# Weights that wait in the caches' buffers, squares added pair by pair, and a new order of streams in a one-core decoder layer

## The chip, the core and the metric

The kernel runs on one core of a Trainium2 chip. The metric is the time of one execution on the device, in microseconds. The kernel before takes 557.04 us (median of three runs, 556.88 to 557.81).

## The reference

One layer of a decoder with two token mixers on 256 new prompt tokens and 64 sampled tokens (8 requests of 8 tokens, each with 1024 cached tokens in pages of 128), 1024 channels wide, everything in fp32. Cut to what matters:

```python
h = rms_norm(x, g_mix)
qa, ka, va, qs, ks, vs, ga, gs = split(h @ w_in)          # 512 x6, 1024 x2
qa, ka = rope(qa), rope(ka)
o_a = moba(qa, past_a + ka, past_a + va)     # softmax over the own block and the best 3 blocks of 256
o_s = stick_breaking(qs, past_s + ks, past_s + vs)
merged = sigmoid(ga) * (o_a @ w_branch_moba) + sigmoid(gs) * (o_s @ w_branch_sb)
x = x + merged @ w_out
h2 = rms_norm(x, g_ffn)
x = x + (silu(h2 @ w_gate) * (h2 @ w_up)) @ w_down        # 2816 wide
y = rms_norm(x, g_final)
return y, ka, va, ks, vs
```

## The kernel before

Channels lie on the 128 partitions, the 320 tokens along the free dimension, so the input x is a tile of 128 x 8 x 320 and a weight for 128 output channels is 128 x 1024, 0.5 MB. Every dense product is made three times in a reduced form of fp32: x and each weight are split into a high part (ACT, a cast, L152, tile wh) and a low part (DVE, a subtraction, L153, tile wl), and TensorE adds up high x high, low x high and high x low (`acc`, L185, and `products`, L344), 24 matmuls of 320 columns for one tile of 128 output channels (named dps). A raw weight comes by DMA from the SP queue into one of three buffers (wr, L157), and its parts lie in three buffers each.

The first norm is not applied to x but to the products. `load_x` loads x in four pieces of two k-tiles and the first two weights in halves, splits them as they land, squares x (ACT, L316), adds the squares (DVE, L319, L321) and `rsqrt` sums them over the channels with TensorE (cs, L261), takes the root (ACT, L262) and a Newton step (DVE, L263 to L267). `first_norm` spreads the result over the partitions with TensorE (rb, L275). The first two dense tiles are computed side by side, in four steps of two k-tiles, and wait with the third (`NORM`) until the norm is there; their rotation (ACT, L363) and the next tiles follow.

Until some 265 us the kernel mixes six streams of work: d (dense tiles of q, k and v and the first branch product), g (gates), s (scores against the cached keys, S, L571, then the own scores, own, L620, zo, L622, and the softmax, pown, L645), a (values, po, L696), e (ends) and p (attention of the prompt). The string `ORDER` says which stream takes the next step; TensorE, POOL and SP run in the order in which the program is written, while a scheduler orders ACT and DVE. After every step `Loads.feed` issues what has become possible: it splits waiting weights as long as fewer than three split ones are unused, and starts the loads that stand next in the order of need, weights on SP and keys on SP (kr, L533, four DMAs of 0.25 MB), values on POOL (vr, L541, an indirect DMA of 1 MB). Keys and values share a ring of eight buffers (tag cr) of 1 MB. Before it issues a page of values, POOL reads an element of the key tile that was loaded second to last (seen, L540), so that pages do not overtake keys.

Behind that come the gated branches, the output projection with the second norm, the feed-forward part and `last_norm`: for each half of the tokens it sums the squares with TensorE (rb, L861), makes r on ACT (L870, L871) and DVE (L875, L876), copies r to PSUM (rstd, L877), multiplies the x that was scaled by g_final (xg, L873 for the last tile) by r in three products (L865), on DVE or POOL, and stores each (L866).

Of the kernel before, what the change touches and what calls it, by code (L numbers as in the profile page):

```python
# [10 lines left out]
ALU = mybir.AluOpType  # L11
# [27 lines left out]
FIRST = "wwwwc"  # L39
# [13 lines left out]
    "dddddddsdddsdddsdaspaddsadasegaddaapedsapdpsggdaapepaaddgpds"  # L53
    "spepdgddpsagasapggegapaapgpsseggpggpdsagdasaaedgaaded"
# [7 lines left out]
class Loads:  # L62
# [4 lines left out]
    def __init__(self, needs, parts, split):  # L67
# [4 lines left out]
        self.ready = 0  # L72
# [8 lines left out]

    def split_one(self):

        self.got["w"].append(self.parts())
        self.split(*self.got["w"][-1], self.raw.pop(0))
        self.ready += 1

# [7 lines left out]
    def feed(self):  # L95

        while self.raw and self.ready - self.used["w"] < WB:
            self.split_one()
        left, held, begun = [], set(), 0
        for kind, load in self.todo:  # L100
            if kind == "c":
                free = self.begun["c"] - self.used["c"] < RB and begun < PACE
            else:
                free = self.begun["w"] - self.ready < WR
# [35 lines left out]
class Net:  # L140
# [14 lines left out]
    def load_weights(self, src, n):  # L155
        raw = self.wpool.tile([P, 1024], F32, name=self.uid("wr"), tag="wr", bufs=WR)
# [121 lines left out]
    def load_x(self):  # L278
# [10 lines left out]
        w = [self.wpool.tile([P, 1024], F32, name=self.uid("wr"), tag="wr", bufs=WR) for i in range(2)]  # L289
        parts = [self.weight_parts() for i in range(2)]  # L290
        load_w = lambda i, h: nc.sync.dma_start(w[i][:, half[h]], self.I["w_in"][i][:, 4 * h:4 * h + 4])
        load_x = lambda g: nc.sync.dma_start(x[:, 2 * g:2 * g + 2], self.I["x"][:, 2 * g:2 * g + 2])
        nc.scalar.dma_start(self.small, self.I["c_small"])
        for h in range(2):
            load_x(2 * h)
            load_w(0, h)
            load_w(1, h)
# [3 lines left out]
        self.loads.begin(FIRST[:2])  # L301

        nc.scalar.activation(self.warm, self.ones[:, 0:1], AF.Sqrt)
        for k in range(KD):
# [3 lines left out]
            if k % 4 < 2:  # L308
                nc.scalar.activation(parts[k % 4][0][:, half[h]], w[k % 4][:, half[h]], AF.Copy)
# [25 lines left out]
    def products(self, tiles, n):  # L335
# [3 lines left out]
        for k in range(0, KD, n):  # L339
            for low in range(2):  # L340
                for w, ps in zip(ws, pss):
# [727 lines left out]
```

## Time and profile before

| what | value |
|---|---|
| median of the runs | 557.04 us (556.88 to 557.81) |
| profiled execution | 557.35 us, of which its span 555.6 us |
| granted clock of TensorE, mean | 0.996 |
| TensorE busy | 540.8 us (97%) |
| DVE, ACT, POOL busy | 328.7, 270.4, 50.4 us |
| DMA | 138.86 MB, mean 250 GB/s |
| chain that ended last | TensorE 88%, DMA 5%, DVE 3%, ACT 3% |

TensorE is busy nearly all the time, and what is not its work lies in a few waits and at the two ends. Busy time counts a matmul up to its modelled end, so that a share of 97% does not say that matmuls follow each other as closely as they can: from 265 to 545 us they start 0.146 us apart (1913 in 280.00 us). A line number in a row is that of the kernel before.

### The profile page before, as it was taken

What the parts mean: (1) busy time and instruction counts of PE and PEld (TensorE: products, weight loads), DVE (VectorE), ACT (ScalarE), POOL (GpSimd) and SP (SyncE); (2) the same over time, 40 slices, a digit from 0 to 9 for tenths busy, and PEclk for the clock granted to TensorE, in tenths of its full rate; (3) what the DMA queues carried; (4) which work ended last, traced back from release to release, by engine and by line L of the source; (5) the groups of instructions that cost most, each with busy time, mean ns of one, the idle gap of its engine ahead of it and who ended that gap; (6) DMA issues with size and microseconds to landing.
All of it is one profiled execution on the core that took longest, in us unless ns stands there. A gap on an engine that the chain in (4) does not pass through costs nothing.

```text
span 555.6 us, 10933 instructions
## 1 busy us (share of the span) xinstructions
PE 540.8 (97%) x4254; PEld 492.1 (89%) x4254; DVE 328.7 (59%) x599; ACT 270.4 (49%) x488; POOL 50.4 (9%) x74
## 2 busy tenths in 40 slices
PE   8899999999999999999999999999999999999993
PEld 6788677878878778878999999999999999999993
DVE  5786655464468537663877666555555565443432
ACT  6894555526675346532545464444443333353421
POOL 0001211150034202320000000000000000000001
PEclk9999999999999999999999999999999999999998
DMA  6999999999799999995585444445544444545512
GB/s 229 380 390 368 352 384 416 399 415 403 251 354 360 422 392 339 403 377 189 171 323 172 144 140 152 152 152 152 150 145 149 148 146 137 154 145 142 169 36 94
DMA packets 45427, 138.86 MB, mean 250 GB/s; under 512 B 5184, under 2 KB 7488, under 8 KB 41152
## 3 DMA queue, kind: packets, MB, share of 16 engines
q1 hardware_dynamic: 40336, 104.06, 54.5%
q0 software_dynamic: 4608, 33.56, 14.9%
q8 instruction: 33, 0.54, 0.4%
q10 hardware_dynamic: 432, 0.56, 0.3%
q14 instruction: 18, 0.15, 0.1%
HBM read 134.22 MB, written 3.93 MB: 249 GB/s over the span
## 4 chain that ended last, share of the span: by engine, by line
PE 88%; DMA 5%; DVE 3%; ACT 3%; issue 1%; POOL 0%; DVEq 0%; SPq 0%; ACTq 0%; POOLq 0%
PE dps L185 56%; PE dps L344 16%; PE po L696 5%; PE S L571 4%; DMA wr<-in_w_in 2%; DMA vr<-in_cv,small 2%; PE dps L388 1%; PE dps L518 1%; PE dps L463 1%; PE tp L504 1%; DVE wl L153 1%; PE tp L672 1%; ACT wh L152 1%; DMA small<-in_c_small 1%; ACT sq L316 0%
## 5 line engine op out<-in xcount | busy, mean ns | idle before, releaser
L152 ACT ACTIVATE wh<-wr 128x1024 fp32r<-128x1024 f32 (+1 forms) x122 | 127.1, 1045 | 180.1 <-issue 105.3
L153 DVE TENSOR_TENSOR wl<-wr,wh 128x1024 fp32r<-128x1024 f32 (+1 forms) x122 | 146.9, 1205 | 67.7 <-ACT wh L152 67.1
L185 PE MATMUL dps<-x1h,wh 128*128 128x320 f32 x352 | 109.0, 310 | 0.0
L185 PE MATMUL dps<-x1l,wh 128*128 128x320 f32 x352 | 108.8, 309 | 0.0
L185 PE MATMUL dps<-x1h,wl 128*128 128x320 f32 x352 | 108.8, 309 | 0.0
L344 PE MATMUL dps<-xs,wh 128*128 128x320 f32 x256 | 78.0, 318 | 0.3 <-ACT xs L306 0.3
L344 PE MATMUL dps<-xl,wh 128*128 128x320 f32 x256 | 76.1, 310 | 0.2 <-DVE xl L307 0.2
L185 PEld LDWEIGHTS dps<-x1h,wh 128*128 128x128 f32 x352 | 66.1, 188 | 0.1
L185 PEld LDWEIGHTS dps<-x1l,wh 128*128 128x128 f32 x352 | 66.1, 188 | 0.0
L185 PEld LDWEIGHTS dps<-x1h,wl 128*128 128x128 f32 x352 | 66.1, 188 | 0.0
L185 PE MATMUL dps<-fl,wh 128*128 128x320 f32 x176 | 54.4, 309 | 0.0
L185 PE MATMUL dps<-fh,wl 128*128 128x320 f32 x176 | 54.4, 309 | 0.0
L185 PE MATMUL dps<-fh,wh 128*128 128x320 f32 x176 | 54.4, 309 | 0.0
L344 PEld LDWEIGHTS dps<-xs,wh 128*128 128x128 f32 x256 | 48.1, 188 | 3.9 <-issue 2.4
L344 PEld LDWEIGHTS dps<-xl,wh 128*128 128x128 f32 x256 | 48.1, 188 | 1.0 <-DVE xl L307 0.6
L344 PE MATMUL dps<-xs,wl 128*128 128x320 f32 x256 | 43.1, 309 | 0.0
L344 PEld LDWEIGHTS dps<-xs,wl 128*128 128x128 f32 x256 | 39.0, 188 | 0.0
L541 POOL DMA_INDIRECT vr<-in_cv,small x32 | 36.0, 1124 | 19.1 <-PE po L696 8.6
L696 PE MATMUL po<-vr,pt 128*32 128x256 f32 x512 | 32.0, 381 | 1.1 <-DMA vr<-in_cv,small 1.1
L185 PEld LDWEIGHTS dps<-fh,wh 128*128 128x128 f32 x176 | 33.0, 188 | 0.0
L185 PEld LDWEIGHTS dps<-fl,wh 128*128 128x128 f32 x176 | 33.0, 188 | 0.0
L185 PEld LDWEIGHTS dps<-fh,wl 128*128 128x128 f32 x176 | 33.0, 188 | 0.0
(202 smaller groups left out, 845.8 us busy)
## 6 DMA issues: line engine op xcount, KB each, us to landing
kr<-in_ck SPq DMA_DIRECT2D x128, 256.0 KB
wr<-in_w_ff SPq DMA_DIRECT2D x44, 512.0 KB
wr<-in_w_in SPq DMA_DIRECT2D x30, 512.0 KB
wr<-in_w_down SPq DMA_DIRECT2D x16, 448.0 KB
wr<-in_w_v SPq DMA_DIRECT2D x8, 512.0 KB
wr<-in_w_b SPq DMA_DIRECT2D x8, 512.0 KB
wr<-in_w_out SPq DMA_DIRECT2D x8, 512.0 KB
wr<-in_w_down SPq DMA_DIRECT2D x8, 512.0 KB
```

Source lines behind the costliest of these rows:

```text
L152: self.nc.scalar.activation(hi, raw, AF.Copy)
L153: self.nc.vector.tensor_tensor(lo, raw, r32(hi), ALU.subtract)
L185: nc.tensor.matmul(ps, w, x, start=first and i == 0, stop=last and i == len(todo) - 1)
L344: self.nc.tensor.matmul(ps, a, x, start=k + low + i == 0, stop=low == 1 and k + n == KD and i == n - 1)
L388: nc.tensor.matmul(ps, self.xs[:, k], w[k][j], start=k + j == 0, stop=k + j == KD)
L463: nc.tensor.matmul(S[e][:, i], q[r, 2 * u + i, half * P:half * P + P], k[r, 2 * u + i, half * P:NP_], start=True, stop=True)
L504: nc.tensor.transpose(tp[:, i * P:(i + 1) * P], src, self.ident)
L518: nc.tensor.matmul(po[r, i, :NP_ if kt else P], t["v"][:, kt, c0:c0 + HD], mv, start=kt == 1, stop=kt == 0)
L541: self.nc.gpsimd.indirect_dma_start(out=raw.rearrange("p a b -> p (a b)"), out_offset=None, in_=self.I[f"cv{br}"], in_offset=bass.Indirect ...
L571: nc.tensor.matmul(S[r], self.block(QS, x, hp), raw[x][:, :, hp * P:(hp + 1) * P], start=i == 0, stop=i == 1)
L672: nc.tensor.transpose(tp[:, i * P:(i + 1) * P], pf[:, 4 * g + i], self.ident)
L696: nc.tensor.matmul(po[r], PT[j][:, r], v[:, c:c + 256], start=j == 0, stop=j == 8)
```

## The change

It has five parts. First, `FIRST` and `begin_two`: two pairs of early weights (the third and fourth of w_in, and the sixth and seventh) are loaded into buffers of the caches' ring, two weights in one buffer (wc), beside the three of their own; a buffer goes back to the ring when both weights in it are split. The constants (cosine, sine, identity, diagonal) are issued between them. Second, the squares: two of the four are made among the first casts, and they are added pair by pair, in three additions of 128 x 640. Third, x lies in DRAM as four contiguous pieces, and is read so again later. Fourth, a new `ORDER`, and queries of the second branch are made when that is possible at another tile. Fifth, the end: DVE scales the last tile, the products are in another order, and all stores but the last go over the SP queue.

```diff
-FIRST = "wwwwc"
+FIRST = "WwkccWw"
+SIDE = 2
+SQUARES = (), (), (), (0,), (), (), (), (2,), (), (4, 6)
...
-    "dddddddsdddsdddsdaspaddsadasegaddaapedsapdpsggdaapepaaddgpds"
-    "spepdgddpsagasapggegapaapgpsseggpggpdsagdasaaedgaaded"
+    "ddddddddsdsdddsdadspdddasapeddasdgpdspaasegaggaaapdepaddpdsa"
+    "spepdgdpsagpdapaseggapgpaagsseggpggpdsagddasaaegaaded"
...
+    def begin_two(self, tile):
+        self.begun["c"] += 1
+        for raw in [tile[:, 2 * i:2 * i + 2].rearrange("p a b -> p (a b)") for i in range(2)]:
+            i = [kind for kind, _ in self.todo].index("w")
+            self.todo.pop(i)[1](raw)
+            self.raw.append(raw)
+            self.guests.append(raw)
...
     def split_one(self):
...
+        if any(raw is g for g in self.guests):
+            self.away += 1
+            self.used["c"] += self.away % 2 == 0
...
-        load_x = lambda g: nc.sync.dma_start(x[:, 2 * g:2 * g + 2], self.I["x"][:, 2 * g:2 * g + 2])
+        load_x = lambda g: nc.sync.dma_start(x[:, 2 * g:2 * g + 2], self.I["x"][g])
...
-        self.loads.begin(FIRST[:2])
+        for c in FIRST:
+            if c == "k":
+                self.constants3()
+            elif c == "W":
+                self.loads.begin_two(self.craw.tile([P, 4, 512], F32, name=self.uid("wc"), tag="cr", bufs=RB))
+            else:
+                self.loads.begin(c)
...
+        def square(k):
+            nc.scalar.activation(sq[:, k:k + 2], x[:, k:k + 2], AF.Square)
+            if k:
+                nc.vector.tensor_add(sq[:, :2], sq[:, :2], sq[:, k:k + 2])
         for k in range(KD):
...
+            for j in SQUARES[k]:
+                square(j)
         self.loads.are_split(parts)
-        self.loads.split_one()
-        for k in range(0, KD, 2):
-            nc.scalar.activation(sq[:, k:k + 2], x[:, k:k + 2], AF.Square)
+        if SIDE < WB:
+            self.loads.split_one()
+        for j in SQUARES[9]:
+            square(j)
...
-        for n in (4, 2):
-            nc.vector.tensor_add(sq[:, :n], sq[:, :n], sq[:, n:2 * n])
...
+            e = KD - 1
+            nc.vector.tensor_scalar(xg[:, e], self.x1[:, e], self.g_fin[:, e:e + 1], None, op0=ALU.mult)
             for h in range(2):
                 nc.scalar.activation(r[h], ps[h], AF.Abs_reciprocal_sqrt, scale=1.0 / D)
                 nc.scalar.activation(w[h][0], r[h], AF.Square)
-            e = KD - 1
-            nc.scalar.activation(xg[:, e], self.x1[:, e], AF.Copy, scale=self.g_fin[:, e:e + 1])
             for h in range(2):
...
-                product(nc.gpsimd, nc.scalar, h, 5, 8, r[h])
+                product(nc.vector, nc.sync, h, 0, 2, rb[h] if h else r[h])
                 if h == 0:
-                    product(nc.vector, nc.sync, 0, 0, 2, r[0])
-            for h, e0, e1 in (0, 2, 5), (1, 0, 2), (1, 2, 5):
-                product(nc.vector, nc.sync, h, e0, e1, rb[h])
+                    product(nc.vector, nc.sync, h, 2, 5, rb[h])
+                product(nc.gpsimd, nc.sync, h, 5, 8, r[h])
+            product(nc.vector, nc.scalar, 1, 2, 5, rb[1])
```

How the instructions stand is seen best from the rows of an engine. ACT at the start, before (xs is the cast of x, sq a square, wh a weight's high part, rot a rotation, rtok the root of the norm):

```order
L306 ACTIVATE xs<-x_105,small 128x320 x2
L152 ACTIVATE wh_151<-wr_122 128x1024
L316 ACTIVATE sq_106<-x_105 128x640 x4
L317 ACTIVATE xs<-xl 128x8x64
L152 ACTIVATE wh_258<-wr_124 128x1024
L363 ACTIVATE rot_388<-dps_208 32x320 x4
L363 ACTIVATE rot_396<-dps_209 32x320 x4
L152 ACTIVATE wh_262<-wr_174 128x1024
L152 ACTIVATE wh_335<-wr_176 128x1024
L262 ACTIVATE rtok<-cs_323,small 128x3
L152 ACTIVATE wh_424<-wr_266 128x1024
```

And after:

```order
L342 ACTIVATE wh_111<-wr_108 128x512
L338 ACTIVATE xs<-x_105,small 128x320 x2
L333 ACTIVATE sq_106<-x_105 128x640
L173 ACTIVATE wh_192<-wc_122 128x1024
L333 ACTIVATE sq_106<-x_105 128x640 x2
L355 ACTIVATE xs<-xl 128x8x64
L173 ACTIVATE wh_275<-wc_122 128x1024
L401 ACTIVATE rot_403<-dps_225 32x320 x4
L401 ACTIVATE rot_411<-dps_226 32x320 x4
L173 ACTIVATE wh_279<-wr_125 128x1024
L284 ACTIVATE rtok<-cs_340,small 128x3
```

One square has moved between the casts of x (above these rows) and one behind the last of them, the other two stand behind the first whole weight (wh_192), and one whole weight (wh_279) instead of two stands between the rotations and the root.

TensorE, before, where the second half of the first value product begins (S are the scores of the next pair, po the value product):

```order
L344 MATMUL dps_1092<-xs,wl_843 128x320 x8
L571 MATMUL S_1126<-kr_768,QS_195 32x512 x2
L571 MATMUL S_1126<-kr_802,QS_195 32x512 x2
...
L696 MATMUL po_1031<-vr_893,pt_935 32x256 x2
L696 MATMUL po_1031<-vr_916,pt_935 32x256 x2
```

After, where the same value product begins, with its first half:

```order
L382 MATMUL dps_1100<-xs,wl_846 128x320 x8
L735 MATMUL po_1132<-vr_654,pt_907 32x256 x2
L735 MATMUL po_1132<-vr_693,pt_907 32x256 x2
...
L610 MATMUL S_1165<-kr_741,QS_212 32x512 x2
L610 MATMUL S_1165<-kr_781,QS_212 32x512 x2
...
L735 MATMUL po_1132<-vr_866,pt_914 32x256 x2
L735 MATMUL po_1132<-vr_895,pt_914 32x256 x2
```

Before, the first half came two dense tiles earlier; after, the first half stands behind these tiles, and only the scores stand between the halves.

ACT, before, at the second v weights (v and vt are the copies of v, QS that of the queries, pown the exponential of the own scores, p that of the others):

```order
L383 ACTIVATE v_204<-dps_699,rtok 128x256
L602 ACTIVATE QS_195<-qT_202 64x4x2x8
L152 ACTIVATE wh_687<-wr_534 128x1024
L390 ACTIVATE vt_799<-dps_782,rtok 64x256
L152 ACTIVATE wh_691<-wr_601 128x1024
L645 ACTIVATE pown_749,st_604<-zo_745,st_604 64x8 x2
L647 ACTIVATE p_603,st_604<-S_605,st_604 128x2x8x16 x2
```

And after:

```order
L421 ACTIVATE v_221<-dps_657,rtok 128x256
L173 ACTIVATE wh_635<-wr_494 128x1024
L641 ACTIVATE QS_212<-qT_219 64x4x2x8
L421 ACTIVATE v_221<-dps_755,rtok 128x256
L684 ACTIVATE pown_722,st_642<-zo_718,st_642 64x8
L173 ACTIVATE wh_683<-wr_547 128x1024
L684 ACTIVATE pown_722,st_642<-zo_718,st_642 64x8
L686 ACTIVATE p_641,st_642<-S_643,st_642 128x2x8x16 x2
```

The high part of the fourth v weight, wh_687 before and wh_683 after, stood two rows and another weight in front of pown and now stands behind its first instruction.

## Rows read from the trace of the kernel before

**Rows 1.** Two stretches: busy time of each engine, granted clock, DMA share, rate.

```profile
core 0: us, PE busy (x) PEld busy (x) DVE busy (x) ACT busy (x) POOL busy (x), PEclk, DMA share, GB/s
95.00:140.00 45.00, 45.00 (x438) 36.38 (x440) 22.90 (x56) 21.46 (x48) 9.96 (x16) 1.00 1.02 405
265.00:545.00 280.00, 280.00 (x1913) 279.80 (x1912) 163.69 (x242) 120.29 (x173) 0.00 (x0) 1.00 0.48 151
```

**Rows 2.** TensorE's waits: line, for whom, us in total, times, longest.

```profile
PE cs L261 <- DVE sq L321: 1.4, 1, 1.4
PE po L696 <- DMA vr<-in_cv,small: 1.1, 2, 0.8
...
PE rb L275 <- PE dps L344: 0.8, 1, 0.8
```

**Rows 3.** ACT at the start, in order of time: start, us, operation, [idle before].

```profile
7.83 1.47 ACT L306 ACTIVATE xs<-x,small 128x320 fp32r<-128x320 f32 x3 [1.17 <-DMA x<-in_x]
...
12.93 2.60 ACT L316 ACTIVATE sq<-x 128x640 f32<-128x640 f32 x4
...
20.56 2.01 ACT L152 ACTIVATE wh<-wr 128x1024 fp32r<-128x1024 f32 x2
...
26.39 1.28 ACT L327 ACT_TABLE_LOAD   x1
```

**Rows 4.** DVE in order of time at the start.

```profile
15.57 1.49 DVE L319 TENSOR_TENSOR sq<-sq 128x1280 f32<-128x1280 f32 x1 [1.28 <-ACT sq L316]
...
18.18 0.82 DVE L319 TENSOR_TENSOR sq<-sq 128x640 f32<-128x640 f32 x1
19.03 0.49 DVE L321 TENSOR_TENSOR sq<-sq 128x320 f32<-128x320 f32 x1
...
21.66 2.36 DVE L153 TENSOR_TENSOR wl<-wr,wh 128x1024 fp32r<-128x1024 f32 x2 [1.03 <-ACT wh L152]
```

**Rows 5.** TensorE in order of time, value products and the tiles behind them.

```profile
77.48 0.60 PE L696 MATMUL po<-vr,pt 128*32 128x256 f32 x4
...
80.70 0.41 PE L344 MATMUL dps<-xs,wh 128*128 128x320 f32 x1
...
91.37 0.63 PE L696 MATMUL po<-vr,pt 128*32 128x256 f32 x4
...
94.63 0.41 PE L344 MATMUL dps<-xs,wh 128*128 128x320 f32 x1
...
101.86 1.93 PE L696 MATMUL po<-vr,pt 128*32 128x256 f32 x32
...
104.16 0.33 PE L664 MATMUL tp<-ident,pown 128*128 128x128 f32 x1
```

**Rows 6.** POOL in order of time, before the late value pages.

```profile
65.06 1.40 POOL L540 COPY seen<-kr 1x1 f32<-1x1 f32 x1 [13.69 <-DMA kr<-in_ck]
```

**Rows 7.** The chain of waits from 60 to 95 us: start us, us, what.

```profile
82.06 10.68 DMA vr<-in_cv,small
```

**Rows 8.** The tail in order of time.

```profile
547.61 0.33 DVE L875 SCALAR_TENSOR_TENSOR v<-w,rb 128x160 f32<-128x160 f32 x1 [1.47 <-ACT w L871]
...
548.05 0.55 ACT L873 ACTIVATE xg<-x,small 128x320 f32<-128x320 f32 x1
548.34 0.49 DVE L865 TENSOR_TENSOR out<-xg,r 128x320 f32<-128x320 f32 x1
...
548.73 2.35 POOL L865 TENSOR_TENSOR out<-xg,r 128x480 f32<-128x480 f32 x2 [301.33 <-ACT xg L873]
```

**Rows 9.** Two stretches of the tail.

```profile
550.50:551.00 0.50, 0.00 (x0) 0.00 (x0) 0.29 (x1) 0.18 (x1) 0.50 (x1) 1.00 0.30 115
551.00:554.00 3.00, 0.00 (x0) 0.00 (x0) 0.76 (x2) 0.00 (x0) 0.08 (x1) 0.60 0.97 363
```

**Rows 10.** DVE and ACT around the own scores of the first pair.

```profile
51.72 0.17 DVE L622 TENSOR_TENSOR zo<-own,small 128x8 f32<-128x8 f32 x1 [0.57 <-PE dps L388]
...
55.13 0.30 ACT L645 ACTIVATE pown<-zo,st 64x8 f32<-64x8 f32 x1 [0.51 <-DVE st L643]
```

More of the change, by code (lines that the diff above doesn't have):

```diff
@@ L95, in feed @@
     def feed(self):
+        ready = self.ready - self.away
         while self.raw and self.ready - self.used["w"] < WB:
             self.split_one()
+        if not WLAG:
+            ready = self.ready - self.away
         left, held, begun = [], set(), 0
@@ L103, in feed @@
             else:
-                free = self.begun["w"] - self.ready < WR
+                free = self.begun["w"] - ready < WR
             if free and kind not in held:
@@ L153, in split, with load_weights @@
         self.nc.vector.tensor_tensor(lo, raw, r32(hi), ALU.subtract)
-    def load_weights(self, src, n):
-        raw = self.wpool.tile([P, 1024], F32, name=self.uid("wr"), tag="wr", bufs=WR)
+    def load_weights(self, src, n, raw=None):
+        if raw is None:
+            raw = self.wpool.tile([P, 1024], F32, name=self.uid("wr"), tag="wr", bufs=WR)
         self.nc.sync.dma_start(raw[:, :n], src)
@@ L288, in load_x @@
         half = slice(0, 512), slice(512, 1024)
-        w = [self.wpool.tile([P, 1024], F32, name=self.uid("wr"), tag="wr", bufs=WR) for i in range(2)]
-        parts = [self.weight_parts() for i in range(2)]
+        w = [self.wpool.tile([P, 1024], F32, name=self.uid("wr"), tag="wr", bufs=WR) for i in range(SIDE)]
+        parts = [self.weight_parts() for i in range(SIDE)]
         load_w = lambda i, h: nc.sync.dma_start(w[i][:, half[h]], self.I["w_in"][i][:, 4 * h:4 * h + 4])
-        load_x = lambda g: nc.sync.dma_start(x[:, 2 * g:2 * g + 2], self.I["x"][:, 2 * g:2 * g + 2])
+        load_x = lambda g: nc.sync.dma_start(x[:, 2 * g:2 * g + 2], self.I["x"][g])
         nc.scalar.dma_start(self.small, self.I["c_small"])
@@ L295, in load_x @@
             load_x(2 * h)
-            load_w(0, h)
-            load_w(1, h)
+            for i in range(SIDE):
+                load_w(i, h)
             load_x(2 * h + 1)
@@ L308, in load_x @@
             if k % 4 < 2:
-                nc.scalar.activation(parts[k % 4][0][:, half[h]], w[k % 4][:, half[h]], AF.Copy)
+                for i in range(1, SIDE) if k % 4 else [0]:
+                    nc.scalar.activation(parts[i][0][:, half[h]], w[i][:, half[h]], AF.Copy)
             if k % 4 == 1:
@@ L339, in products @@
         for k in range(0, KD, n):
-            for low in range(2):
-                for w, ps in zip(ws, pss):
-                    pairs = [(w[low][:, j], x[:, j]) for j in range(k, k + n) for x in (self.xh, self.xl)[:2 - low]]
-                    for i, (a, x) in enumerate(pairs):
-                        self.nc.tensor.matmul(ps, a, x, start=k + low + i == 0, stop=low == 1 and k + n == KD and i == n - 1)
+            steps = [(low, i) for low in range(2) for i in range(len(tiles))]
+            for low, i in steps if k + n < KD else sorted(steps, key=lambda v: v[1]):
+                w, ps = ws[i], pss[i]
+                pairs = [(w[low][:, j], x[:, j]) for j in range(k, k + n) for x in (self.xh, self.xl)[:2 - low]]
+                for j, (a, x) in enumerate(pairs):
+                    self.nc.tensor.matmul(ps, a, x, start=k + low + j == 0, stop=low == 1 and k + n == KD and j == n - 1)
         return pss
@@ L409, in gen_qk @@
             if f == 0:
-                side_by_side = self.products([0, 1], 2)
-            todo.append((which, hp, side_by_side.pop(0) if f < 2 else self.project(f)))
+                side_by_side = self.products(range(SIDE), 2)
+            todo.append((which, hp, side_by_side.pop(0) if f < SIDE else self.project(f)))
             if f < NORM:
@@ L767, in out_proj @@
         self.rstd2 = rstd = q.tile([P, T], F32, name="rstd2")
-        nc.sync.dma_start(x1, I["x"])
+        for g in range(4):
+            nc.sync.dma_start(x1[:, 2 * g:2 * g + 2], I["x"][g])
         acc = self.acc1 = q.tile([P, 1, T], F32, name="acc1")
@@ L962, in build @@
                 self.page_rows()
-                self.constants3()
-                self.loads.begin(FIRST[2:])
                 self.work = mid.enter_context(pool("work"))
```

17 lines of the change are left out of this document (11 added, 6 removed).

## The prediction

> **What bounds the kernel now.** I read the stretches first, then TensorE's waits, then the order in time at the places that the waits name. From 265 to 545 us TensorE has no gap at all, 280.00 us for 1913 matmuls, 0.146 each; from 95 to 140 us it has none either, while the DMA engines are full at 405 GB/s [rows 1]. So the time is TensorE's work plus its few waits plus the tail behind 545 us, and a change that keeps the matmuls can only win or lose waits. The list of waits has, of those that the change touches, the column sums behind the squares (1.4 us), the value pages (1.1 us on TensorE's own list) and the broadcast of the norm (0.8 us, put down to TensorE, in truth behind a chain on ACT and DVE) [rows 2]. I price these places and the tail, and then look for what the new order could hold up.
>
> **The start: squares and norm.** Before, ACT makes all four squares only from 12.93 us on, in 2.60 us, 0.65 each [rows 3]. DVE then adds 128x1280 (15.57, 1.49 us), a weight's low part comes between, then 128x640 (18.18, 0.82) and 128x320 (19.03, 0.49) [rows 4]. The sum is there at 19.52; the third tile was through at 17.9. After, the first square stands behind the cast of k=3 and the second behind that of k=7. ACT has work without a gap from 7.83 us to the squares, so its casts of the second half come a square later, 0.65: the two tiles side by side end some 0.6 later, the third begins near 15.0 instead of 14.4 and ends near 18.5 (24 matmuls are 3.5). The adds become three of 128x640 (0.82 each) instead of 1.49 + 0.82, 0.15 more, but the first lies beside ACT's next weight. On DVE I get: first add 13.05 to 13.87, low part 14.1 to 15.3 (1.2 each, 2.36 for two [rows 4]), two adds to 16.95, low part 17.05 to 18.25, last sum 18.75. The column sums start 0.8 earlier and wait 0.2 instead of 1.4.
>
> What decides is the next link, the norm. Before, ACT casts two weights (20.56, 2.01 us) between the rotations and the root [rows 3], and DVE makes two low parts (21.66, 2.36 us) before the Newton step [rows 4]. After, one cast and one low part stand there. Up to the rotations' end ACT has the same work as before. One cast and one low part less bring the end of the low parts from 24.0 to about 22.7, and the broadcast 1.3 us earlier than 24.9. The fourth tile ends near 22.9, so a wait of 0.7 stays. **Term 1: -1.3 us**, bounds -0.9 (the square in front of the casts costs more than its row) and -2.2 (with rival a).
>
> Two pairs of weights go into cache buffers. They lend two of the eight until about 18 and 30 us; the first product with keys comes behind the eighth tile, past 36, so I cost the loan at nothing. Uncovered it would be a tile of keys, 1.05 MB at 405 GB/s, 2.6 us.
>
> **The value pages.** The page's 1.1 us understates them. An undisturbed second half of a value product (40 matmuls) takes 2.30 us to the next tile, 101.86 to 104.16, so a first half (32) takes 1.84. The second half at 77.48 took until 80.70, 3.22, and the first half at 91.37 until 94.63, 3.26 [rows 5]: 0.92 + 1.42 = 2.3 us lost. The pages were late because POOL, which issues them, stood 13.69 us until 65.06 for a tile of keys [rows 6], and because a page then needs up to 10.68 us from issue to landing [rows 7]. In the new order the first value products stand behind three more dense tiles, near 75 instead of 66.6 us; the second half follows at 78.7, and the next come as a double at 108. I counted the megabytes that must have landed before each tile (0.52 a weight, 2.1 a pair of tiles of keys or values) against 390 GB/s: the two tiles that waited had 24.1 and 29.4 MB ahead of them and some 11 us of slack in that count; after, the second half has 24.7 MB at a time 3.5 us later, and the double 35.7 MB with 14 us. The buffers of its four tiles come free by 81, 27 us ahead. I take both waits as gone: **term 2: -2.3 us**, bounds 0 and -2.3.
>
> **The tail.** Before, ACT scales the last tile (548.05, 0.55) after both roots, and POOL's product waits for it until 548.73; DVE idles 1.47 us before 547.61 [rows 8]. After, DVE scales in that hole (0.55 by ACT's row; uncovered it would cost that), and POOL can start at 548.4, when the first half's factor is there. But the end is set by the stores: the engines are at 115 GB/s from 550.5 to 551.0 and at 363 from 551.0 to 554.0 [rows 9], some 1.1 MB that nothing makes shorter. What moves their start is the second and third store: DVE's 128x480 product follows at once after its first (end 549.5 for 549.98), POOL's is 0.3 earlier. **Term 3: -0.4 us**, bounds 0 and -0.5 (the half-idle stretch).
>
> **The rest of the order.** ACT has two more table loads (1.28 us each [rows 3]), near 113 to 137 us, where the weights' casts run some 13 us ahead of their use: nothing; without that lead, 2.6. Small shifts (a gate's sigmoid ahead of a cast, the later softmax) I put at +0.2.
>
> Sum: -1.3 - 2.3 - 0.4 + 0.2 = -3.8 us on the profiled execution's 557.35 (its span of 555.6 and 1.75 around it): 553.55. That run lies 0.31 above the median of the runs, 557.04; medians are compared, so **553.3**.
>
> **Rivals.** (a) *The contiguous pieces of x land together.* ACT waits 1.17 us for x until 7.83 [rows 3], on a piece issued long before; each piece now is one block instead of rows with a pitch of 10 KB. If the slowest engines' share comes with the others', the casts start up to 0.9 earlier, and with them squares and norm: 0.4 to 0.9 more, 552.6. Against it: the weights' halves beside them keep their layout.
>
> (b) *The page waits only move.* POOL still waits for keys before it issues. If the same 2.3 us appears at 79, 108 or 127 us, terms 1 and 3 remain: 555.6.
>
> (c) *POOL takes SBUF from DVE in the tail.* In the trace POOL's product starts at 548.73, while DVE's product with both inputs in SBUF runs until 548.83 [rows 8]: an overlap of 0.10 us and no hold. After, both become free within 0.1 us of each other. If POOL (2.35 us for two) came first and DVE had to wait out its 1.18, DVE's first two products would end at 550.0 and 550.6 and term 3 would be gone: 553.7. The Trainium skill says so of them: by SBUF — State Buffer, on the port pair that DVE and GpSimd share (its rules on contention), a DVE instruction with two SBUF inputs and a GpSimd one that reads SBUF exclude each other for the whole of the one that began first. By that rule the sum is -3.4. The overlap in the row speaks against it, but POOL's times are rough.
>
> (d) *The own scores hold a v weight.* In the new ACT order the cast of the fourth v weight (wh_683) stands behind the exponential of the own scores (pown), and that behind zo on DVE. Before, zo ran at 51.72, only when TensorE's following tile ended, and pown at 55.13, 3.4 later [rows 10]. If zo again waits for the end of what follows its matmuls, the cast comes 3.4 us after its buffers are free: +3.4, 556.7. If it starts with the end of its own matmuls, 4.7 us of matmuls cover it. Later ones of its kind showed no such lag, so I count on the latter.
>
> (e) *Slower: the second double starves.* The double at 108 holds four buffers until 112.8; two of the four tiles of the next double, at 127, can be issued only then, at 113.3 and 114.6. With 10.68 us to land [rows 7] they are there at 125.3, 2 us ahead. But the engines are full [rows 1]: if the two tiles behind them, two of keys and three weights share the wire evenly with the four pages from 107.5 on, 9.9 MB at 405 GB/s land at 132, 4.9 us late: -3.8 + 4.9, 558.1. It makes the kernel slower from a landing at 131 on. For it: 10.68 us was such sharing. Against it: in the order of issue the four stand ahead, and that puts them at 124.
>
> **Chances.** Forecast 0.53, (a) 0.14, (b) 0.14, (c) 0.05, (d) 0.08, (e) 0.06. A measurement of this kernel tells about 0.2%, 1.1 us, from no change. Faster, below 555.9: the forecast but for 0.02, (a), (c), two thirds of (b) and a part of (d), 0.82 in all; the same 0.12, from the rest of (b), (d) and (e); slower 0.06. The range holds the forecast with its bounds and (a) to (c): 551.9 to 555.8; outside are (d), (e) and a little of (b). The forecast's own is 552.5 to 554.3.
>
> **What would show it.** Right: the wait for the column sums is under 0.4 us and the fifth tile starts at 24.3 to 24.8 (25.8 before); the value halves take 1.84 and 2.30 us; TensorE has no wait for pages at 108 and 127; the wire is full from about 550.5, counted in a tail that starts 3.4 earlier. Wrong: casts of x more than a square's time later; a wait of over 2 us for a low part near 52; pages at 127; a product of POOL or DVE in the tail that is a microsecond longer.

## The result: 550.6 us, outside the forecast range on the fast side

The changed kernel takes 550.58 us (median of four runs, 550.09 to 551.65) where the kernel before took 556.97 in the runs beside it: a ratio of 0.9884, with an interval from 0.9866 to 0.9903, so 6.4 us less. The forecast was 553.3, and its range ended at 551.9. The profiled execution of after took 550.09 us, its span 548.3; against the span of before it lies 7.26 us lower, of which some 0.9 is the luck of the two executions that were profiled (0.4 above its median before, 0.5 below it after). On another chip (s_after, in the last group) the same kernel won only 1 to 2 us; where it lost the rest is told there.

| what | before | after |
|---|---|---|
| median | 556.97 us | 550.58 us |
| span of the profiled execution | 555.6 us | 548.3 us |
| TensorE busy | 540.8 us | 538.0 us |
| fifth dense tile starts | 25.83 us | 23.57 us |
| second branch product starts | 265.56 us | 258.84 us |
| last sums over channels (rb) start | 545.39 us | 538.67 us |
| from there to the end of the span | 10.19 us | 9.65 us |

The last four lines place the gain: 2.26 us at the start, 4.46 more before the second branch product, nothing in the 280 us behind it, 0.54 in the tail. First the stretches of after, with the columns of [rows 1].

```profile
core 0: us, PE busy (x) PEld busy (x) DVE busy (x) ACT busy (x) POOL busy (x), PEclk, DMA share, GB/s
95.00:140.00 45.00, 45.00 (x460) 36.41 (x459) 23.52 (x58) 29.30 (x67) 9.15 (x16) 1.00 1.02 411
258.00:538.00 280.00, 280.00 (x1912) 279.80 (x1912) 163.79 (x242) 120.25 (x173) 0.00 (x0) 1.00 0.49 154
```

The dense part behind 258 us is the same to a matmul, 1912 for 1913 in 280.00 us. From 95 to 140 us the wire (the 16 DMA engines) is as full as before, 411 GB/s for 405, and TensorE is busy all the time in both; the 460 matmuls for 438 are of other sizes in part, since the order differs. Next TensorE's waits; those left out are of 0.2 us.

```profile
PE warm L253 <- DVE ones L245: 0.9, 1, 0.9
PE tp L711 <- DVE p L624: 0.5, 1, 0.5
PE dps L382 <- ACT wh L342: 0.3, 1, 0.3
...
PE rb L297 <- PE dps L382: 0.2, 1, 0.2
```

Against [rows 2] the column sums' wait (1.4) and the pages' (1.1) are gone, and the broadcast's 0.8 has become 0.2. A wait of 0.9 us for a weight's low part, which the list of before also has, is gone too. The start, first ACT, in order of time, beside [rows 3].

```profile
7.08 1.02 ACT L338 ACTIVATE xs<-x,small 128x320 fp32r<-128x320 f32 x2 [0.24 <-DMA x<-in_x]
8.00 0.72 ACT L333 ACTIVATE sq<-x 128x640 f32<-128x640 f32 x1
...
11.48 0.72 ACT L333 ACTIVATE sq<-x 128x640 f32<-128x640 f32 x1
...
13.05 1.35 ACT L333 ACTIVATE sq<-x 128x640 f32<-128x640 f32 x2
...
19.44 1.06 ACT L173 ACTIVATE wh<-wr 128x1024 fp32r<-128x1024 f32 x1
20.52 0.26 ACT L284 ACTIVATE rtok<-cs,small 128x3 f32<-128x3 f32 x1
```

Then DVE, beside [rows 4], and TensorE.

```profile
12.78 0.81 DVE L335 TENSOR_TENSOR sq<-sq 128x640 f32<-128x640 f32 x1
...
14.65 1.74 DVE L335 TENSOR_TENSOR sq<-sq 128x640 f32<-128x640 f32 x2
...
17.45 0.48 DVE L357 TENSOR_TENSOR sq<-sq 128x320 f32<-128x320 f32 x1
...
20.53 1.23 DVE L174 TENSOR_TENSOR wl<-wr,wh 128x1024 fp32r<-128x1024 f32 x1 [1.49 <-ACT wh L173]
```

```profile
17.99 0.83 PE L283 MATMUL cs<-ones,sq 128*128 128x1 f32 x6
...
22.60 1.04 PE L297 MATMUL rb<-ident,rtok 128*128 128x128 f32 x6 [0.16 <-PE dps L382]
23.57 0.42 PE L382 MATMUL dps<-xs,wh 128*128 128x320 f32 x1
```

The sum of squares ends at 17.93 us where it ended at 19.52, TensorE takes it without a wait, and with one low part instead of two ahead of the Newton step the broadcast stands ready 0.16 us after TensorE. ACT's first cast behind its wait for x starts at 7.08 instead of 7.83. The value products of after, with the columns of [rows 5]:

```profile
74.61 1.93 PE L735 MATMUL po<-vr,pt 128*32 128x256 f32 x32
76.36 1.90 PE L610 MATMUL S<-kr,QS 128*32 128x512 f32 x16
78.08 1.91 PE L735 MATMUL po<-vr,pt 128*32 128x256 f32 x32
...
80.35 0.37 PE L502 MATMUL dps<-kT,qT 64*128 64x128 f32 x1
...
106.73 3.66 PE L735 MATMUL po<-vr,pt 128*32 128x256 f32 x64
...
110.64 0.61 PE L610 MATMUL S<-kr,QS 128*32 128x512 f32 x4
...
124.49 3.66 PE L735 MATMUL po<-vr,pt 128*32 128x256 f32 x64
...
128.51 0.33 PE L703 MATMUL tp<-ident,pown 128*128 128x128 f32 x1
```

A first half now takes 1.75 us and a second 2.27; the doubles take 3.91 and 4.02, the sum of two halves. POOL still stands for keys ahead of the pages, as in [rows 6]:

```profile
64.11 0.23 POOL L579 COPY seen<-kr 1x1 f32<-1x1 f32 x1 [14.20 <-DMA kr<-in_ck]
...
87.83 0.18 POOL L579 COPY seen<-kr 1x1 f32<-1x1 f32 x1 [20.18 <-DMA kr<-in_ck]
```

So the pages are no earlier; the products that need them stand later in the order. The tail, beside [rows 8], all engines:

```profile
539.46 0.39 DVE L910 TENSOR_SCALAR xg<-x,small 128x320 f32<-128x320 f32 x1
...
541.62 0.49 DVE L905 TENSOR_TENSOR out<-xg,r 128x320 f32<-128x320 f32 x1
541.90 1.26 POOL L905 TENSOR_TENSOR out<-xg,r 128x480 f32<-128x480 f32 x1 [297.70 <-DVE r L916]
542.03 0.65 DVE L905 TENSOR_TENSOR out<-xg,rstd 128x480 f32<-128x480 f32 x1
...
543.35 1.20 POOL L905 TENSOR_TENSOR out<-xg,r 128x480 f32<-128x480 f32 x1 [0.19 <-DVE r L916]
```

POOL starts its first product 3.23 us behind the first rb, for 3.34 before (548.73 less 545.39).

### The profile page after: what moved, and what is told of

It is laid out like the page before. It is cut to its first block, busy times and chain, and to the rows that moved or that the text cites. A ratio compares the mean times of both kernels' runs of the same rounds, so it can differ in the third digit from the quotient of the medians.

```text
span 548.3 us, 10933 instructions
## 1 busy us (share of the span) xinstructions
PE 538.0 (98%) x4254; PEld 493.0 (90%) x4254; DVE 329.0 (60%) x601; ACT 272.2 (50%) x489; POOL 44.3 (8%) x74
## 4 chain that ended last, share of the span: by engine, by line
PE 95%; DVE 2%; ACT 1%; DMA 1%; issue 0%; SPq 0%; DVEq 0%; ACTq 0%
PE dps L207 57%; PE dps L382 20%; PE po L735 5%; PE S L610 5%; PE dps L426 1%; PE tp L711 1%; PE dps L502 1%; PE dps L557 1%; PE tp L543 1%; ACT rot L401 1%; DMA wr<-in_w_in 1%; PE tp L748 0%; PE rb L297 0%; PE own L659 0%; DVE out L905 0%; PE cs L283 0%
## 5 line engine op out<-in xcount | busy, mean ns | idle before, releaser
L173 ACT ACTIVATE wh<-wr 128x1024 fp32r<-128x1024 f32 (+1 forms) x118 | 123.0, 1045 | 164.8 <-issue 102.8
L174 DVE TENSOR_TENSOR wl<-wr,wh 128x1024 fp32r<-128x1024 f32 (+1 forms) x118 | 142.0, 1204 | 71.9 <-ACT wh L173 71.8
L580 POOL DMA_INDIRECT vr<-in_cv,small x32 | 33.4, 1044 | 25.5 <-PE po L735 15.7
L610 PE MATMUL S<-kr,QS 128*32 128x512 f32 x256 | 31.7, 595 | 0.0
```

The source lines that it names most:

```text
L173: self.nc.scalar.activation(hi, raw, AF.Copy)
L174: self.nc.vector.tensor_tensor(lo, raw, r32(hi), ALU.subtract)
L580: self.nc.gpsimd.indirect_dma_start(out=raw.rearrange("p a b -> p (a b)"), out_offset=None, in_=self.I[f"cv{br}"], in_offset=bass.Indirect ...
L610: nc.tensor.matmul(S[r], self.block(QS, x, hp), raw[x][:, :, hp * P:(hp + 1) * P], start=i == 0, stop=i == 1)
```

## The experiments

They ran in four groups; the kernels of a group shared a chip and the runs of the kernel before, and ratios are to those (they are not the ratios of the medians, and the two can differ by 1 us). In short: the new order earns most, the start earns nothing without it, and the parts' sum is only half of what the whole gave on two other chips; the whole was not run on the chip of the parts.

### The parts alone

**The pieces of x alone** (p_pieces).

```diff
-        load_x = lambda g: nc.sync.dma_start(x[:, 2 * g:2 * g + 2], self.I["x"][:, 2 * g:2 * g + 2])
+        load_x = lambda g: nc.sync.dma_start(x[:, 2 * g:2 * g + 2], self.I["x"][g])
...
```

> The kernel before with one edit: x lies in DRAM as four contiguous pieces and is read so. Theory A (the parts add up, and the pieces let a piece's slowest share land some 0.8 us earlier, as the trace after shows: 7.05 for 7.81): ACT waits about 0.3 instead of 1.17 us for x, the fifth dense tile starts 0.6 to 0.9 earlier than 25.83, time -0.8 us. Theory B (the late shares come from the weights' halves on the same wire, the pieces change nothing, and the earlier landing after is the new queue's doing): 0.

Measured: 1.0005 (0.9989 to 1.0020). ACT's cast behind x starts at 7.81 us, 7.83 before. By itself the layout does nothing that shows, within some 1 us.

**The start alone** (p_start): pairs of weights and squares, with x in rows, the old order and the old end. It also has an edit that the part on the change does not name: in the last step of the two tiles side by side (`products`), the first tile is finished before the second.

```diff
-FIRST = "wwwwc"
+FIRST = "WwkccWw"
+SIDE = 2
+SQUARES = (), (), (), (0,), (), (), (), (2,), (), (4, 6)
...
```

> The kernel before with the pairs of weights in the caches' buffers, the constants between them and the squares pair by pair; x in rows, old order of streams, old tail. Theory A: the fifth dense tile starts 1.3 us earlier (24.5), the waits at 53, 77 and 91 us stay, time -1.3 us. Theory B (the free SP queue brings keys and pages earlier too, and takes a part of the page waits): -2.5 to -3.5 us, the value halves at 77 and 91 near 1.84 and 2.30.

Measured: 1.0019 (0.9999 to 1.0039), though the fifth tile starts at 24.55. TensorE in order of time, where the first scores stand, and the stretch behind it, with the columns of [rows 1]:

```profile
37.40 3.15 PE L609 MATMUL S<-kr,QS 128*32 128x512 f32 x16 [2.02 <-ACT QS L640]
```

```profile
38.00:42.00 4.00, 4.00 (x22) 2.02 (x13) 2.72 (x7) 2.51 (x6) 0.00 (x0) 0.57 0.93 321
```

The scores wait 2.02 us for the copy of the queries (QS), which ACT makes at 37.09, behind rotations and two weights. Behind that stand the granted clock is 0.57 on the mean of 4 us, most of it at the lower of its two levels, 1.2 GHz, and 16 matmuls take 3.15 us for 1.92 after. From the fifth tile to the prompt's scores it is 42.57 us for 39.75 before, so what the start won is spent. Its tail is longer too, 10.84 us for 10.19 from the first rb to the end, as in the two runs of the start with the exchange (10.85 in both); why is open.

**The order alone**, with the queries' new place (p_order).

```diff
-    "dddddddsdddsdddsdaspaddsadasegaddaapedsapdpsggdaapepaaddgpds"
+    "ddddddddsdsdddsdadspdddasapeddasdgpdspaasegaggaaapdepaddpdsa"
...
```

> The kernel before with the new order of streams alone (and the queries that follow it). Theory A: the page waits of 2.3 us go, the wait for a v weight's low part (1.0 us) goes, since the own scores no longer stand directly before the samples' v tile, and some 1 us of small waits from 105 to 265 go: -4 us. Theory B (the order needs the start's earlier loads): page waits or weight waits appear elsewhere and the gain is 2 us or less.

Measured: 0.9942 (0.9923 to 0.9961), 554.07 us for 557.54, 3.5 less, with no wait for a page on TensorE's list, and the column sums' wait of 1.3 us still there. But there is a new one, for the high and the low part of the fourth v weight:

```profile
54.67 0.38 PE L185 MATMUL dps<-wh,xs 128*128 128x256 f32 x1 [0.38 <-ACT wh L152]
55.93 0.39 PE L185 MATMUL dps<-wl,xs 128*128 128x256 f32 x1 [0.88 <-DVE wl L153]
```

ACT casts this weight at 53.56 us, behind pown and three of the exponentials p; in the changed kernel it does so at 49.20, and TensorE does not wait. From the fifth tile to the prompt's scores the order alone takes 40.38 us, the changed kernel 39.21.

**The end alone** (p_tail).

```diff
-            nc.scalar.activation(xg[:, e], self.x1[:, e], AF.Copy, scale=self.g_fin[:, e:e + 1])
+            nc.vector.tensor_scalar(xg[:, e], self.x1[:, e], self.g_fin[:, e:e + 1], None, op0=ALU.mult)
...
```

> The kernel before with the new end alone. Theory A: from the last dense tile's end to the end of the span 9.65 us instead of 10.19, time -0.5 us. Theory C (POOL and DVE hold each other up where both read two inputs from SBUF, and the stores' rate decides): 0 to -0.2.

Measured: 0.9983 (0.9964 to 1.0001), 1.2 us less at the median, with an interval that reaches to nothing. The times do not settle the size. The trace does: from the first rb to the end it is 9.81 us, where the six other profiles with x in rows and the old end, those of the start with the old order apart, have 10.16 to 10.22.

### The whole again, and the two waits taken away otherwise

**The changed kernel** (q_after), no edit.

> The changed kernel again, beside the kernel before on one chip, since the parts were run on another day than it. In the parts' runs TensorE's granted clock fell to its lower level for 3 to 4 us behind a wait of 1.3 us or more (column sums, scores). Theory A (the parts add up: 0, +1.2, -3.5, -1.25): -3.5 us. Theory D (the changed kernel has no wait of 1.3 us left, so its clock never falls, and the start's edits gain only together with the new order): -6 to -7 us, granted clock 1.00 in every stretch up to the tail.

Measured: 0.9880 (0.9852 to 0.9909), 550.31 us.

**The changed kernel with x in rows** (q_rows).

```diff
-        load_x = lambda g: nc.sync.dma_start(x[:, 2 * g:2 * g + 2], self.I["x"][g])
+        load_x = lambda g: nc.sync.dma_start(x[:, 2 * g:2 * g + 2], self.I["x"][:, 2 * g:2 * g + 2])
...
```

> The changed kernel with x in rows of 10 KB pitch again. Theory (pieces gain): 0.6 to 0.9 us slower than the changed kernel. Theory (the landing of x scatters from execution to execution by as much, 7.4 to 8.3 us for the second piece in the runs so far, and the layout does nothing): the same as the changed kernel within 0.4 us.

Measured: 0.9887 (0.9862 to 0.9912), 550.79 us; ACT's cast behind x at 7.14 us for 7.22 in q_after. The 0.5 us to q_after lies between the two expectations: the layout is at most some half a microsecond of the gain. 0.16 of it is in the tail, 9.82 us for 9.66.

**Before, with TensorE kept at work ahead of the column sums** (q_filled): three matmuls of ones, 256 columns each, whose result is not used.

```diff
+        if len(acc) == 1 and acc[0] is self.sq and FILL:
+            for _ in range(FILL):
+                nc.tensor.matmul(ps[:, 64:320], self.ones.to_broadcast([P, P]), self.ones.to_broadcast([P, 256]), start=True, stop=True)
...
```

> The kernel before with three more matmuls of 256 columns on TensorE in the wait ahead of the column sums, into unused columns of their PSUM tile (their result is not used). They fill some 1.3 us in which TensorE waits anyway. Theory D (the clock falls because TensorE stood still): no stretch of the start with a clock under 1.00, the fourth tile in 3.5 us, time -0.6 to -1.6 us against the kernel before where that one falls. Rival (the clock falls for another reason, or costs nothing, since the norm's chain is the longer one): 0.

Measured: 1.0003 (0.9984 to 1.0023), at the median 556.41 us for 557.02. In p_pieces, which waits as before does, the granted clock is 0.57 on the mean from 20 to 24 us, behind the wait for the column sums; here it is 1.00. But the broadcast, in order of time:

```profile
24.35 1.04 PE L279 MATMUL rb<-ident,rtok 128*128 128x128 f32 x6 [0.83 <-PE dps L348]
25.32 0.41 PE L348 MATMUL dps<-xs,wh 128*128 128x320 f32 x1
```

TensorE waits 0.83 us for the norm instead. So most of what the lower clock takes here is hidden behind the chain on ACT and DVE, and not all of it: in the four profiles with the old start in which the clock fell (p_pieces, p_order, p_tail, q_lag0) it is 18.40 to 18.43 us from ACT's cast behind x to the fifth tile, and where it did not fall 17.94 (here) and 18.00 (the profiled execution of before, whose clock stayed at 1.00 behind the same wait). The fall costs 0.4 us, too little for this run's times to tell from none. The rest needs a shorter chain.

**Before, with POOL not waiting for keys** (q_lag0).

```diff
-LAG = 2
+LAG = 0
```

> The kernel before with POOL not waiting for the key tile loaded second to last (no seen). Theory: the page waits at 77, 91 and 184 us (2.8 to 3.8 us in four traces) come from POOL's wait, and fall by more than half: -1.5 to -3 us. Rival: the ring of eight buffers and the full wire set when pages land; then the waits stay and pages overtake keys: scores wait instead, 0 or slower.

Measured: 1.0141 (1.0115 to 1.0168), 8 us slower. TensorE's waits:

```profile
PE S L571 <- DMA kr<-in_ck: 7.4, 3, 4.6
```

The list has no wait for a page any more; the keys are waited for, for 7.4 us. The wire is full (409 GB/s from 70 to 95 us), and an earlier page is a later key. The new order does the other thing: it leaves the transfers and moves the need.

### Start and order together, and the place of the first scores

**The start alone with the first scores one dense tile later** (r_start_swap), to take p_start's wait for the queries away.

```diff
-    "dddddddsdddsdddsdaspaddsadasegaddaapedsapdpsggdaapepaaddgpds"
+    "ddddddddsddsdddsdaspaddsadasegaddaapedsapdpsggdaapepaaddgpds"
```

> The start's edits alone (x in rows, old tail), with one exchange in the old order of streams: the first scores stand one dense tile later. In the run without the exchange these scores waited 2.0 us for the queries (ACT copies them behind five weights' casts), and the clock fell to its lower level behind that wait: 3.4 us in its trace. Theory D (that wait ate the start's gain): no such wait, no fall there, 3 us less than without the exchange, 2 us less than the kernel before. Theory A (the start's edits gain nothing by themselves): within 1 us of the kernel before.

Measured: 1.0035 (1.0022 to 1.0047), 2.1 us slower than before. The wait for the queries is gone and the fifth tile starts at 23.88, but the second half of the first value product, TensorE in order of time:

```profile
76.19 0.63 PE L734 MATMUL po<-vr,pt 128*32 128x256 f32 x4
79.36 1.97 PE L734 MATMUL po<-vr,pt 128*32 128x256 f32 x26 [2.55 <-DMA vr<-in_cv,small]
...
82.54 0.64 PE L382 MATMUL dps<-xs,wh 128*128 128x320 f32 x1
```

This second half takes 6.35 us instead of 2.30. TensorE comes to the page earlier, the page does not, and behind the stand the granted clock is 0.50 from 81 to 84 us (a dense matmul's row then has 0.47 us for 0.31). Again as s_start_swap, in the last group:

> The start's edits with the exchange, old order otherwise. In its trace the fifth dense tile started at 23.9, as after, but the value half at 76 us took 6.4 us: pages land when the wire lets them, and TensorE only waits longer when it comes earlier. If that holds, again within 2 us of the kernel before, the wait for pages over 3 us; if it was an accident, 2 us faster than the kernel before.

Measured: 1.0038 (1.0019 to 1.0058), the same product 7.06 us.

**Start and order, old end, x in rows** (r_start_order); **the changed kernel with the old end** (r_old_tail).

```diff
-                product(nc.vector, nc.sync, h, 0, 2, rb[h] if h else r[h])
+                product(nc.gpsimd, nc.scalar, h, 5, 8, r[h])
...
```

> The start's edits and the new order of streams; x in rows, old tail. Theory D: -5.5 to -6 us against the kernel before (the order's 3.5 and the start's 2.2), clock 1.00 up to the tail. Theory A (sum of the single runs): -2.3 us.

> The changed kernel with the end of the kernel before. By the traces (9.65 against 10.19 us from the last dense tile to the end of the span): 0.5 us slower than the changed kernel. By the run of the tail alone: 1.2 us slower. Theory C (the stores' rate decides): 0 to 0.2.

Measured: 0.9968 (0.9944 to 0.9991) and 0.9948 (0.9921 to 0.9976). Both had runs near 553.4 and others up to 559.5; the next group says where.

**The changed kernel with the first scores one dense tile earlier** (r_swap_back).

```diff
-    "ddddddddsdsdddsdadspdddasapeddasdgpdspaasegaggaaapdepaddpdsa"
+    "dddddddsddsdddsdadspdddasapeddasdgpdspaasegaggaaapdepaddpdsa"
```

> The changed kernel with the one exchange undone: the first scores one dense tile earlier, as before, all else as changed. Theory D: the scores wait 2 us for the queries, the clock falls behind it, 3 to 3.5 us slower than the changed kernel. Theory A: within 0.5 us of it.

Measured: 1.0013 (0.9987 to 1.0038). The 2.0 us for the queries are back, with waits of 0.9 and 0.4 us for the v weight behind them, as in p_order, and stands of 2.6 us in all at the own scores, of which the next group tells more. From the fifth tile to the prompt's scores this profile takes 44.29 us for 39.21 after, so that the one letter costs 5.1 us there. The rest of what it lost lies at the own scores, where the kernels of this chip without the exchange lose time too.

### What makes the changed kernel's time vary

> The changed kernel once more, on the same chip as the next three. Theory F (in the runs of the start with the order and of the old tail TensorE stood for nothing that the profile shows at the own scores near 113 us, 0.5 to 4.3 us, because of the chip or the day, not the edit): here too 552 to 556 us, with such a stand. Theory G (their edits bring it): 550.3 us, no stand, and the others stand.

> The changed kernel with the old end, beside the changed kernel. Theory F: 0.5 us slower than the changed kernel in the same call. Theory G: 3 us slower, standing near 113 us.

> The start's edits and the new order, x in rows, old tail, beside the changed kernel. Theory F: 0.5 to 1 us slower than it. Theory G: 4 to 6 us slower.

No new edits: the changed kernel, r_old_tail's kernel and r_start_order's on another chip. Measured: 0.9963 (0.9939 to 0.9986) with runs from 552.59 to 558.54; 0.9986 (0.9964 to 1.0008); 0.9963 (0.9942 to 0.9985). On this chip the changed kernel won 1.1 us at the median and 2.1 by the ratio, in its first runs and in the second group 6.4 and 6.7 at the median. TensorE in s_after, in order of time:

```profile
112.70 0.42 PE L659 MATMUL own<-kT,QS 128*32 128x8 f32 x8
113.53 0.22 PE L659 MATMUL own<-kT,QS 128*32 128x8 f32 x3 [0.41 <-issue]
114.24 0.17 PE L659 MATMUL own<-kT,QS 128*32 128x8 f32 x1 [0.48 <-issue]
114.96 0.25 PE L659 MATMUL own<-kT,QS 128*32 128x8 f32 x4 [0.55 <-issue]
116.39 0.42 PE L748 MATMUL tp<-ident,o 128*128 128x128 f32 x2 [1.18 <-issue]
...
117.80 0.31 PE L382 MATMUL dps<-xl,wh 128*128 128x320 f32 x1 [0.84 <-issue]
```

And two stretches of the same profile:

```profile
112.00:118.00 6.00, 2.53 (x33) 1.62 (x24) 1.35 (x4) 0.47 (x1) 4.31 (x7) 1.00 1.03 431
118.00:122.00 4.00, 4.00 (x19) 4.00 (x19) 2.80 (x14) 0.88 (x4) 0.00 (x0) 0.57 1.01 418
```

The first of them in the first profile of the changed kernel (after):

```profile
112.00:118.00 6.00, 6.00 (x64) 5.68 (x57) 4.92 (x19) 3.16 (x6) 3.17 (x5) 1.00 1.01 425
```

TensorE stands in the run of small own-score matmuls for nothing that the trace shows, then works at a granted clock of 0.57 on the mean; its second double starts at 130.83 us for 124.49. Meanwhile the wire is full at 431 GB/s and POOL issues six pages back to back; but so it is in after, at 425 GB/s and with six pages, where nothing stands. All six profiles of the start with the new order on this chip and that of the third group lose at this one place. From the scores ahead of it (110.64 us in after) to the transposes behind it (tp, 112.58) it is 1.93 to 2.08 us in after, q_after and p_order; it is 3.92 in r_old_tail, 6.65 in r_start_order, 7.04 in r_swap_back, 5.41 in s_after, 4.50 in s_old_tail and 3.28 in s_start_order. In r_old_tail and s_start_order, executions of 553.54 and 553.72 us, most of it shows as longer instructions (scores of 3.13 and 3.25 us for 1.90, in r_old_tail also own scores of 1.08 us for some 0.3), and the list of waits has 0.3 us of it and nothing. The three kernels have the same order and start; they differ in the end and in x's layout, and their medians lie within 1.3 us, while the same changed kernel lies 6 us apart between chips. So the spread goes with executions and chips, not with these edits. That the supply of instructions comes late over the full wire is a suspicion, and the trace speaks rather against it: the block of instructions that is moved ahead of this place starts at 109.69 us in after and at 110.20 in s_after, and takes 1.04 and 1.05 us. The cause stays open.

## Why the prediction was wrong

The profiled spans differ by 7.26 us. By the prediction's own steps:

| step | forecast | measured |
|---|---|---|
| squares and norm, counted from ACT's cast behind x to the fifth tile | -1.3 | -1.5 (18.00 to 16.49) |
| arrival of x, ACT's cast at 7.08 for 7.83 | 0 (rival a: 0.4 to 0.9) | -0.75 |
| from the fifth tile to the prompt's scores | 0 | -0.54 |
| the two late value halves | -2.3 | -2.3 |
| a third late half | not seen | -0.5 |
| the rest up to the second branch product | +0.2 | -1.1 |
| tail | -0.4 | -0.54 |

**The step that failed is the last term of the sum, "the rest of the order", put at +0.2**, together with the value term's count of two late halves. The two terms forecast -2.1 us. What the new order does behind the prompt's scores measured -3.9 (the -2.3, -0.5 and -1.1 of the table): from there to the last sums over the channels it is 479.8 us before, 475.9 after and 476.0 in p_order, which has the new order alone. By the times the order alone gave 3.5 us, by its interval 2.2 to 4.3, and that with the 1.3 us for the v weight against it. A part of the difference stood in the trace of before, TensorE in order of time:

```profile
184.25 2.22 PE L696 MATMUL po<-vr,pt 128*32 128x256 f32 x30
186.10 0.39 PE L696 MATMUL po<-vs,pto 128*32 128x256 f32 x2
186.30 0.39 PE L696 MATMUL po<-vr,pt 128*32 128x256 f32 x2
...
187.05 1.20 PE L504 MATMUL tp<-ident,z 128*128 128x128 f32 x9
```

That half takes 2.80 us for 2.30, its last two matmuls on a page behind two on another tile, and in the profiles of p_pieces, p_start and p_tail, which have the old order, 3.52, 3.81 and 3.63. In the trace of before it shows as no idle time, so the list of waits does not hold it (in the three others it has 0.63 to 0.93 us there); I looked for late halves only where that list pointed. So before's own profile has 0.5 us of it where the others have 1.2 to 1.5. The other 1.1 us I separated only in part: counted from the start of each to the start of what follows, all value products together take 35.4 us before and 32.3 in after and p_order, so that 0.3 of it is theirs as well; the rest is spread over other instructions. The -0.54 is a wait of some 1 us (0.9 on the list) for a low part at 52 us in the profiled execution of before, gone after, against 0.5 new at the own scores: zo stood then for TensorE's later matmuls [rows 10], and p_pieces, p_tail and q_filled, with the same order there, show no such wait. That was one execution's accident.

**Term 1 was right.** From ACT's cast behind x to the fifth tile it is 18.00 us before (17.94 to 18.43 in the six profiles with the old start), and 16.49 to 16.51 in all twelve with the new one: 1.5 us, 0.2 over the forecast, which put the broadcast's wait at 0.7 us where 0.16 stayed. Against the four profiles whose clock fell it is 1.9, so that the profile of before understates the usual cost of its start. The rest of the 2.26 at the start is the arrival of x. Rival (a) had the size; its cause is not shown: p_pieces and q_rows leave the layout half a microsecond at most. The cast behind x starts anywhere from 7.15 to 8.37 us with the old start and from 6.74 to 8.06 with the new one; among the twelve it is at 7.22 on the mean with pieces and at 7.59 with rows, six each, 0.4 apart where each group spreads over 0.8 us or more. So much of these 0.75 us is the execution's, and a forecast from one trace could not have had it.

**Term 2 did as said at its two places, by the mechanism given.** The starts were forecast as 75, 78.7, 108 and 127 us and came at 74.61, 78.08, 106.73 and 124.49. Rival (b) fell: q_lag0 shows that waits do move when the transfers are moved, but here the need was moved. Rival (e) fell, but by little: by the events of the trace the first double's last page landed at 106.07, 0.66 us ahead, and the second's at 124.68, when that product had begun, yet before its turn.

**Term 3 was right.** It was -0.54 for -0.4 in the profiles. From the first rb to the end, the kernels with x in rows have 10.16 to 10.22 us with the old end (the start with the old order apart) and 9.81 and 9.82 with the new one, those with x in pieces 10.01 and 10.02, and 9.63 to 9.66. So the new end is worth 0.4, and the layout of x, for a reason that no run shows, the other 0.15. The -1.2 of p_tail is the times' scatter; its interval holds 0.4. Rival (c) fell: POOL's first product starts at 541.90, while DVE's with both inputs in SBUF runs until 542.11, and takes 1.26 us for the 1.20 of the second, beside which DVE's reads PSUM. By the Trainium skill, SBUF — State Buffer, section "SBUF: two separate sides", on the shared port pair, such a DVE instruction and a GpSimd one that reads SBUF exclude each other. This trace, with an overlap of 0.21 us, does not show it, as far as spans on POOL can be trusted. Rival (d) fell in the changed kernel: no wait for a v weight's part is listed. But it did not fall for the order: p_order and r_swap_back wait 0.4 and 0.9 us for the parts of just that weight, cast late behind the softmax, though zo is not late there (49.15 us, own scores at 47.67). With the new start and the new place of the first scores together the scheduler casts it earlier.

**The terms were added as if they were independent, and they are not.** Alone, the pieces, the start, the order and the end gave +0.2, +1.2, -3.5 and -1.2 us, -3.3 in all; together they gave 6.4 and 6.7 less in the first runs and the second group, whose profiles show no stand at 112 us. These are other chips than that of the parts, and a chip can move the whole by 5 us, so the sums alone prove little; the traces show where the terms meet. The start's 1.5 us reach the end only if what follows can be early as well: with the old order they go into a wait of 2.0 us for queries (p_start), and with that removed into 4 to 5 us more for a page (r_start_swap). And the order without the start waits 1.3 us for the v weight, which the whole does not. The forecast got the whole start term by luck: the new order happens to hold both cures, the first scores and the first value product each further back, and its text named neither.

What stays open: some 0.8 us of the order's gain, the longer tail of the start with the old order, what the layout of x does, and why TensorE stands at 112 us on some chips.

## What to carry to other kernels

Before counting what a shorter start is worth, look at the next two things that the bottleneck engine will meet earlier, above all a transfer on a full wire: its landing does not move with the engine. Where the wire is full, move the need and not the issue: ordering the products later took 2.3 us of waiting away, issuing the pages earlier turned it into 7.4 us for keys. A wait in one trace is one execution's: compare the same stretch in several profiles before it is priced. And look for lost time by the duration of like groups of instructions, not by the list of waits alone, since a product fed in drips may have no idle time to show.

## What the runs showed of the hardware that was not expected

A stand of TensorE of some 2 us costs more than itself: behind 2.02 us for the queries (granted clock 0.57 from 38 to 42 us) and behind 2.55 us for a page (0.50 from 81 to 84) it worked at the lower of its two clock levels, and 320-column matmuls followed each other 0.27 us apart instead of 0.146. At the column sums, where another chain ends last, such a fall cost 0.4 us; behind that wait of 1.3 us the clock fell in four profiles and stayed at 1.00 in that of before. The small own-score matmuls, 0.17 us each, were the place where TensorE stood for "issue" in steps of 0.4 to 1.2 us beside a wire at 431 GB/s, in the changed kernel's profile on one chip and in neither of its two others, whose nine runs lie between 550.1 and 551.7 us, and whose wire is as full there (425 and 420 GB/s). The arrival of the same piece of x, issued at the same time, spread over 1.6 us.
